# A two-layer decoder trunk on one core: products reordered around late inputs, rows of 1/rms made later, the convolution's diagonal blocks built on chip, eight small matmuls added

## The chip, the core and the metric

The kernel runs on one core of a Trainium2 chip. The metric is device time in microseconds (us) of one execution; lower is better. Engines are named as the profile names them: PE is TensorE's matmul, PEld its weight load, DVE is VectorE, ACT is ScalarE, POOL is GpSimd, SP is SyncE (here it only issues DMAs).

## What is computed

A sequence of 256 positions with 1024 channels passes through two layers, all in float32. Cut to its core:

```python
def half_step_swiglu(h, g, w_gate, w_up, w_down):
    hn = rms_norm(h, g)
    return h + 0.5 * ((silu(hn @ w_gate) * (hn @ w_up)) @ w_down)      # 1024 -> 2816 -> 1024

def conformer_conv_module(hn, w_pw1, b_pw1, conv_w, conv_b, ln_g, ln_b, w_pw2, b_pw2):
    a, gate = split(hn @ w_pw1 + b_pw1, 2)
    u = a * sigmoid(gate)
    u = causal_depthwise_conv(u, conv_w) + conv_b       # 31 taps, 1024 channels
    u = silu(layer_norm(u, ln_g, ln_b))
    return u @ w_pw2 + b_pw2

for layer in range(2):
    h = half_step_swiglu(h, ...)
    hn = rms_norm(h, mix_norm[layer])
    h = h + (hybrid_mixer(hn, ...) if layer == 0 else conformer_conv_module(hn, ...))
    h = half_step_swiglu(h, ...)
return rms_norm(h, final_norm)
```

`hybrid_mixer` is a sparse attention with an indexer beside a short gated convolution, behind one input projection and in front of one output projection.

## The kernel before

Everything is kept transposed: channels on the 128 partitions, the 256 positions along the free axis. A float32 product is made of three single-pass matmuls (`mm3`, lines 260 to 264): a number is split into a high part `hi` and a remainder `lo`, and `wh*ah + wh*al + wl*ah` are summed in PSUM. Each weight tile of 128x2048 is loaded by SP (line 77, buffer `raw`), its high part is made by ACT (line 111, `whi`) and its low part by DVE (line 122, `wlo`). The class `Stream` keeps the order of these tiles: `st.hi(n)` and `st.lo(n)` let ACT and DVE run n tiles ahead of PE, and a new load is issued when a `wlo` is done.

The order of work is written out by hand and is the program's order on each engine; each engine takes its queue strictly in order. A planner (`Side`) decides only between which products the small pieces of the attention and the convolution's taps are put, by costs that the code gives it (`did_pe`, `did_dve`).

Four feed-forward halves (`ffn`, numbered 0 to 3) carry most of the time; the hybrid mixer stands behind the first, the conformer behind the third. What the change touches:

- **1/rms.** The scale 1/rms of a normalisation is not applied to the input but to the products. `norm_cols` (lines 303 to 321) sums squares with small matmuls (line 313), DVE adds epsilon, POOL takes the power -0.5 (line 320, tile `rc`); `row_of` (lines 323 to 330) turns this column into a row with two matmuls (line 326) and ACT copies it to `rstd`. DVE multiplies the finished products by `rstd` when it takes them out of PSUM (lines 344, 351, 963, 968).
- **Start of ffn 1 to 3** (line 398): the products of the first two tiles run over inputs `xh[0..5]` first and over `xh[6..7]` afterwards, because the last pieces of x come late (ACT line 286, DVE line 287).
- **The conformer's convolution.** Channel tiles 0 and 1 are convolved by DVE: 30 taps each, one instruction a tap (line 930). Tiles 2 to 7 are convolved on PE (`conv_pe`, lines 882 to 891): 32 matmuls a tile in four column groups of 32, whose weights are diagonal 32x32 blocks (`W4`). The host packs these blocks and they are loaded by DMA, 512 KB a tile, three by SP ahead of the products and three by ACT between its other work (line 870). Their other operand `U4` is four shifted copies of the gated input u, written to DRAM by an ACT-issued DMA (line 877) and read back by four SP-issued DMAs (line 880) for each pair of tiles.
- **Behind it** comes the layer norm over 1024 channels: `shift_row` (line 907) makes a rough mean from two tiles on PE, DVE subtracts it (lines 901, 913), squares and sums are gathered on ACT, POOL and DVE (lines 916, 1021 to 1033), `cols` (line 921) sums them over channels on PE, and after the power on POOL (line 1053) two rows are made on PE (line 1058). Only then can the second pointwise product start (line 1074 on ACT makes its first input).

## Time and profile before

| | us |
|---|---|
| median of 3 runs | 957.34 |
| lowest and highest of the 3 | 947.97 and 966.21 |
| the profiled execution, its own time | 947.35 |
| its span in the trace | 945.6 |

The profile shows one execution, the 947.35 one. The page gives busy time and idle time of each engine; the list of waits says who waited for whom; the timeline gives start and duration of each instruction, with the idle time in front of it and what ended it in square brackets; the table of stretches gives busy time of each engine in a stretch, the number of instructions in it, and the clock that was granted to PE (1.00 is 2.4 GHz, 0.50 is 1.2 GHz).

### The profile page before, as it was taken

How to read it: one execution, taken by the hardware profiler on the slowest of the kernel's cores; microseconds unless marked ns; L12 is line 12 of the kernel's file. 1: busy time of each engine (PE TensorE's matmuls, PEld its weight loads, DVE VectorE, ACT ScalarE, POOL GpSimd, SP SyncE). 2: the span in 40 equal slices, each digit the busy share in tenths (PEclk: the TensorE clock that was granted, in tenths of full speed). 3: DMA queues.
4: the chain of work that ended last, by engine and by line, in shares of the span. 5: the costliest groups of instructions: out<-in, count | busy, mean ns of one | idle time of the engine just before them, and what ended most of it. 6: DMA issues, size and time to landing. Idle time of an engine off the chain costs nothing. (4 is left out here: it accounts for less than half of the span.)

```text
span 945.6 us, 18509 instructions
## 1 busy us (share of the span) xinstructions
PE 926.0 (98%) x8166; PEld 903.8 (96%) x8166; DVE 613.0 (65%) x684; ACT 445.6 (47%) x504; POOL 93.9 (10%) x77
## 2 busy tenths in 40 slices
PE   8999999999999999999999999999987999999997
PEld 8999999989989999999999999999964999999997
DVE  6776656669776766556666565665975776666542
ACT  7554434554664544344544443455441465444441
POOL 1000001233102000002310000023001020000011
PEclk9999999999999999999999999999998999999999
DMA  8565445672245555455755553568773265554641
GB/s 336 219 230 207 153 149 189 235 257 87 90 178 199 218 208 179 141 166 187 271 194 202 187 188 123 184 229 315 213 218 92 90 225 221 179 200 133 188 150 45
DMA packets 32961, 176.71 MB, mean 187 GB/s; under 512 B 3568, under 2 KB 7536, under 8 KB 18928
## 3 DMA queue, kind: packets, MB, share of 16 engines
q1 hardware_dynamic: 31056, 172.02, 52.2%
q10 hardware_dynamic: 1824, 3.50, 1.2%
q8 instruction: 64, 1.05, 0.4%
q14 instruction: 17, 0.14, 0.0%
HBM read 173.58 MB, written 1.93 MB: 186 GB/s over the span
## 5 line engine op out<-in xcount | busy, mean ns | idle before, releaser
L262 PE MATMUL acc<-xh,whi 128*128 128x256 f32 x1632 | 453.7, 278 | 1.5 <-ACT xh L286 1.5
L263 PE MATMUL acc<-xl,whi 128*128 128x256 f32 x1632 | 452.4, 277 | 1.0 <-DVE xl L287 0.7
L264 PE MATMUL acc<-xh,wlo 128*128 128x256 f32 x1632 | 452.0, 277 | 0.0
L122 DVE TENSOR_TENSOR wlo<-raw,whi 128x2048 fp32r<-128x2048 f32 (+2 forms) x175 | 364.7, 2098 | 11.4 <-ACT whi L111 11.3
L111 ACT ACTIVATE whi<-raw 128x2048 fp32r<-128x2048 f32 (+2 forms) x175 | 299.6, 1715 | 150.3 <-PE acc L263 95.5
L262 PEld LDWEIGHTS acc<-xh,whi 128*128 128x128 f32 x1632 | 307.5, 188 | 2.5 <-ACT xh L286 1.8
L263 PEld LDWEIGHTS acc<-xl,whi 128*128 128x128 f32 x1632 | 307.4, 188 | 1.8 <-DVE xl L287 1.8
L264 PEld LDWEIGHTS acc<-xh,wlo 128*128 128x128 f32 x1632 | 307.2, 188 | 0.0
L264 PE MATMUL acc<-hh,wlo 128*128 128x256 f32 x704 | 194.3, 276 | 0.0
L262 PE MATMUL acc<-hh,whi 128*128 128x256 f32 x704 | 194.3, 276 | 0.0
L263 PE MATMUL acc<-hl,whi 128*128 128x256 f32 x704 | 194.3, 276 | 0.0
L262 PEld LDWEIGHTS acc<-hh,whi 128*128 128x128 f32 x704 | 132.2, 188 | 0.0
L263 PEld LDWEIGHTS acc<-hl,whi 128*128 128x128 f32 x704 | 132.2, 188 | 0.0
L264 PEld LDWEIGHTS acc<-hh,wlo 128*128 128x128 f32 x704 | 132.2, 188 | 0.0
L345 ACT ACTIVATE gs<-gs 128x512 f32<-128x512 f32 x44 | 27.9, 634 | 142.4 <-DVE gs L344 142.4
L351 DVE TENSOR_TENSOR us<-acc,rstd 128x512 f32<-128x512 f32 x44 | 30.4, 690 | 93.5 <-PE acc L264 93.5
L300 POOL TENSOR_TENSOR sqsum<-sqsum,sq 128x256 f32<-128x256 f32 x35 | 54.5, 1558 | 144.4 <-ACT sq L292 143.9
L435 DVE SCALAR_TENSOR_TENSOR x<-acc,x 128x256 f32<-128x256 f32 x32 | 13.6, 425 | 80.3 <-PE acc L264 80.3
L286 ACT ACTIVATE xh<-x,par 128x256 fp32r<-128x256 f32 x48 | 23.8, 505 | 81.1 <-DVE x L435 63.0
L344 DVE TENSOR_TENSOR gs<-acc,rstd 128x512 f32<-128x512 f32 x44 | 30.4, 691 | 46.5 <-PE acc L264 40.4
L300 POOL TENSOR_TENSOR sqsum<-sq 128x256 f32<-128x256 f32 x6 | 5.2, 874 | 543.8 <-ACT sq L292 524.5
L287 DVE SCALAR_TENSOR_TENSOR xl<-x,par,xh 128x256 fp32r<-128x256 f32 x48 | 24.2, 512 | 18.7 <-ACT xh L286 18.7
(187 smaller groups left out, 668.3 us busy)
## 6 DMA issues: line engine op xcount, KB each, us to landing
raw<-in_wgu_dram SPq DMA_DIRECT2D x85, 1024.0 KB, 4.8
raw<-in_wdn_dram SPq DMA_DIRECT2D x64, 704.0 KB, 4.2
raw<-in_wp_dram SPq DMA_DIRECT2D x12, 1024.0 KB, 5.0
raw<-in_wcv_dram SPq DMA_DIRECT2D x6, 1024.0 KB, 4.8
raw<-in_wout_dram SPq DMA_DIRECT2D x4, 1024.0 KB, 4.8
u<-ud SPq DMA_DIRECT2D x12, 284.0 KB, 5.4
raw<-in_wgu_dram SPq DMA_DIRECT2D x4, 512.0 KB, 6.9
raw<-in_wzq_dram SPq DMA_DIRECT2D x2, 1024.0 KB, 5.0
```

Source lines behind the costliest of these rows:

```text
L111: self.nc.scalar.activation(hi[:, :n], self.raw[i][:, :n], AF.Copy)
L122: self.nc.vector.tensor_tensor(lo[:, :n], raw[:, :n], hi[:, :n].bitcast(FT), op=OP.subtract)
L262: nc.tensor.matmul(ps, wh, ah, start=start, stop=False, skip_group_check=skip)
L263: nc.tensor.matmul(ps, wh, al, start=False, stop=False, skip_group_check=skip)
L264: nc.tensor.matmul(ps, wl, ah, start=False, stop=stop, skip_group_check=skip)
L286: nc.scalar.activation(xh[:, d], x[:, d], AF.Copy, scale=g)
L287: nc.vector.scalar_tensor_tensor(xl[:, d], x[:, d], g, xh[:, d].bitcast(FT), op0=OP.mult, op1=OP.subtract)
L300: nc.gpsimd.tensor_tensor(total, parts[0], sq, op=OP.add)
L344: nc.vector.tensor_tensor(gs, two(G), bc2(rstd), op=OP.mult)
L345: nc.scalar.activation(gs, gs, AF.Silu)
L351: nc.vector.tensor_tensor(us, two(U), bc2(rstd), op=OP.mult)
L435: nc.vector.scalar_tensor_tensor(x[:, d], ps[:, :S], 0.5, x[:, d], op0=OP.mult, op1=OP.add)
```

## The change

Seven edits, in the order of the diff's core:

1. `settle`: eight matmuls of 32 columns of weights by 256 in the four column groups, their results unused, behind `row_of` of ffn 0; there `row_of` itself stands 24 matmuls later.
2. The start of ffn 1 to 3 runs over inputs 0 to 3, then 4 and 5, then 6 and 7.
3. `row_of` of the hybrid mixer stands behind the second half's products for both position blocks instead of between them; that of the conformer 12 matmuls later.
4. The diagonal blocks are built on chip from 256 more columns of the parameters: one multiplication of an identity pattern with the weights, both broadcast, 128x1024. Tiles 2, 3 and 4 are built by POOL behind `norm_cols`, tiles 5, 6 and 7 by DVE between the taps. The six loads of 512 KB are gone.
5. After the last pointwise product, `st.hi(3)` and `st.lo(1)` become `st.hi(2)`: the high part of one weight tile further ahead is made later.
6. The planner is told of the builds, and so puts other numbers of taps between the other instructions.
7. The sums for the layer norm: tile 6 is now added into the sums by DVE, and `cols` over the gathered sums stands behind the last convolution tile instead of in its middle.

```diff
+    def settle():
+        p = tp()
+        for _ in range(2):
+            for c in range(4):
+                nc.tensor.matmul(p[32 * c:32 * c + 32, :S], ones[:, :32], con[:, :S], start=True, stop=True,
+                                 tile_position=(0, 32 * c))
...
-                for k0, k1 in ((0, 6), (6, 8)):
+                for k0, k1 in ((0, 4), (4, 6), (6, 8)):
...
-                    if u == 1 and j == 0:
+                    if u == 1 and j == 0 and f:
                         rstd = row_of(rc)
                     run(0, 1, 0, 8, False)
+                    if u == 1 and j == 0 and not f:
+                        rstd = row_of(rc)
+                        settle()
...
-                    if h == 1 and b == 0:
+                    if h == 1 and b == 1:
                         rstd = row_of(rc)
...
+            def build_w4(ct, eng):
+                W4[ct] = cp.tile([128, 32, 32], FT, name="w4", bufs=3)
+                eng.tensor_tensor(W4[ct], m32[:, None, :].to_broadcast([128, 32, 32]),
+                                  par[:, P_W4 + 32 * ct:P_W4 + 32 * ct + 32][:, :, None].to_broadcast([128, 32, 32]),
+                                  op=OP.mult)
+                if eng is nc.vector:
+                    side.did_dve(1.2)
...
-                        if i == 0 and j == 1 and n == 7:
+                        if i == 0 and j == 1 and n == 11:
                             rstd = row_of(rc)
...
                         rc = norm_cols()
+                        for ct in (2, 3, 4):
+                            build_w4(ct, nc.gpsimd)
...
-                    st.hi()
-                    st.lo(1 if i == 3 else AHEAD)
+                    if (i, j) == (3, 1):
+                        st.hi(2)
+                    else:
+                        st.hi(3 if i == 3 else AHEAD)
+                        st.lo(1 if i == 3 else AHEAD)
...
-                load_w4(ct + 3)
+                build_w4(ct + 3, nc.vector)
...
-            nc.vector.tensor_tensor(sd[:, 0], sd[:, 0], sd[:, 1], op=OP.add)
+            nc.vector.tensor_tensor(sq, sq, q0, op=OP.add)
             conv_out(6, p6)
             last = pairs("sg")
             nc.scalar.activation(last[:, 0], v[:, 6], AF.Square)
-            nc.vector.tensor_tensor(sq, sq, q0, op=OP.add)
+            nc.vector.tensor_tensor(sd[:, 1], sd[:, 1], v[:, 6], op=OP.add)
+            nc.vector.tensor_tensor(sd[:, 0], sd[:, 0], sd[:, 1], op=OP.add)
+            nc.vector.tensor_tensor(sq[:, 1], sq[:, 1], last[:, 0], op=OP.add)
             nc.vector.tensor_tensor(sq[:, 0], sq[:, 0], sq[:, 1], op=OP.add)
             p, p2 = acc(), acc()
-
-            def early():
-                cols(p, sd[:, 0], True, False)
-                cols(p2, sq[:, 0], True, False)
-                cols(p, v[:, 6], False, False)
-                cols(p2, last[:, 0], False, False)
-
-            p7 = conv(7, early)
+            p7 = conv(7)
             conv_out(7, p7)
+            cols(p, sd[:, 0], True, False)
+            cols(p2, sq[:, 0], True, False)
```

PE's queue in ffn 0, where the row of 1/rms is made (`rc` is the column, `con` the constants), before:

```order
L263 MATMUL acc<-xl,whi 128x256
L264 MATMUL acc<-xh,wlo 128x256
L326 MATMUL tp<-con,rc 128x128 x2
L262 MATMUL acc<-xh,whi 128x256
L263 MATMUL acc<-xl,whi 128x256
L264 MATMUL acc<-xh,wlo 128x256
```

and with the change, 24 matmuls further on:

```order
L264 MATMUL acc<-xl,whi 128x256
L265 MATMUL acc<-xh,wlo 128x256
L327 MATMUL tp<-con,rc 128x128 x2
L338 MATMUL tp<-con,ones 32x256 x8
L263 MATMUL acc<-xh,whi 128x256
L264 MATMUL acc<-xl,whi 128x256
```

The row is followed by the eight matmuls of `settle`, then by the next products.

ACT's queue from the last write of u to DRAM on (`w` are the diagonal blocks, `v` the convolution's result), before:

```order
L877 DMA ud<-u 128x2x287
L111 ACTIVATE whi<-raw 128x2048
L985 ACT_TABLE_LOAD
L985 ACTIVATE dummy<-ones 128x1
L899 ACTIVATE v<-acc,par 128x256
L870 DMA w_7861<-in_w_dram 128x1024
L899 ACTIVATE v<-acc,par 128x256
L870 DMA w_7905<-in_w_dram 128x1024
L909 ACTIVATE shift<-tp 128x256
L870 DMA w_7958<-in_w_dram 128x1024
```

and with the change:

```order
L894 DMA ud<-u 128x2x287
L1003 ACT_TABLE_LOAD
L1003 ACTIVATE dummy<-ones 128x1
L914 ACTIVATE v<-acc,par 128x256 x2
L924 ACTIVATE shift<-tp 128x256
L931 ACTIVATE q<-v 128x512
```

The `whi` that stood in front of the two copies of the convolution's results is gone from here, and so are the three loads.

DVE's queue from the last gated input u on (`v<-u,par,v` are taps), before:

```order
L972 SCALAR_TENSOR_TENSOR u<-av,par,sg 128x256 x2
L930 SCALAR_TENSOR_TENSOR v<-u,par,v 128x256 x26
L901 SCALAR_TENSOR_TENSOR v<-acc,par,shift 128x256
L913 TENSOR_TENSOR v<-v,shift 128x512
L122 TENSOR_TENSOR wlo<-raw,whi 128x2048
L901 SCALAR_TENSOR_TENSOR v<-acc,par,shift 128x256
L930 SCALAR_TENSOR_TENSOR v<-u,par,v 128x256 x8
L913 TENSOR_TENSOR v<-v,shift 128x512
```

and with the change:

```order
L987 SCALAR_TENSOR_TENSOR u<-av,par,sg 128x256 x2
L945 SCALAR_TENSOR_TENSOR v<-u,par,v 128x256 x6
L884 TENSOR_TENSOR w_7868<-con,par 128x1024
L945 SCALAR_TENSOR_TENSOR v<-u,par,v 128x256 x6
L884 TENSOR_TENSOR w_7910<-con,par 128x1024
L945 SCALAR_TENSOR_TENSOR v<-u,par,v 128x256 x8
L916 SCALAR_TENSOR_TENSOR v<-acc,par,shift 128x256
L884 TENSOR_TENSOR w_7959<-con,par 128x1024
L928 TENSOR_TENSOR v<-v,shift 128x512
L123 TENSOR_TENSOR wlo<-raw,whi 128x2048
L916 SCALAR_TENSOR_TENSOR v<-acc,par,shift 128x256
L945 SCALAR_TENSOR_TENSOR v<-u,par,v 128x256 x14
```

The same 34 taps stand here, 20 instead of 26 in front of the first result that needs the shift, 14 instead of 8 behind it, and three builds among them.

## Rows read from the trace of the kernel before

**Rows 1.** The page: its first line, and PE's busy time.

```profile
span 945.6 us, 18509 instructions
...
PE 926.0 (98%) x8166; PEld 903.8 (96%) x8166; DVE 613.0 (65%) x684; ACT 445.6 (47%) x504; POOL 93.9 (10%) x77
```

**Rows 2.** A wait of PE: who waits for whom, us in total, times, longest.

```profile
PE tp L326 <- POOL rc L320: 1.0, 3, 0.6
```

**Rows 3.** Timeline of PE in the convolution: start, us, instruction, count, [idle before it].

```profile
705.45 1.13 PE L907 MATMUL tp<-v,ones 128*128 128x256 f32 x4 [2.44 <-ACT v L899]
706.51 3.66 PE L888 MATMUL acc<-u,w 128*32 128x256 f32 x64
716.01 8.15 PE L888 MATMUL acc<-u,w 128*32 128x256 f32 x96 [5.85 <-DVE v L930]
...
732.91 0.38 PE L262 MATMUL acc<-u,whi 128*128 128x256 f32 x1 [0.30 <-ACT u L1074]
```

**Rows 4.** Stretches of 1 us there; the third figure from the end is PE's clock.

```profile
715.00:716.00 1.00, 0.00 (x0) 0.02 (x1) 0.97 (x4) 0.00 (x0) 0.00 (x0) 0.50 0.91 352
...
721.00:722.00 1.00, 1.00 (x16) 0.56 (x12) 0.00 (x0) 0.00 (x0) 0.00 (x0) 0.67 0.00 0
```

**Rows 5.** Timeline of ACT in the convolution.

```profile
701.60 1.91 ACT L111 ACTIVATE whi<-raw 128x2048 fp32r<-128x2048 f32 x1 [10.10 <-DMA raw<-in_wgu_dram]
```

**Rows 6.** DMAs issued from 701 to 705 us, then from 689 to 693 us: KB, us to landing.

```profile
u<-ud SPq DMA_DIRECT2D x4, 284.0 KB, 9.2
...
u<-ud SPq DMA_DIRECT2D x4, 284.0 KB, 4.9
```

**Rows 7.** Timeline of DVE in the convolution.

```profile
692.54 0.69 DVE L968 TENSOR_TENSOR av<-acc,rstd 128x512 f32<-128x512 f32 x1 [3.17 <-PE acc L264]
...
694.14 10.38 DVE L930 SCALAR_TENSOR_TENSOR v<-u,par,v 128x256 f32<-128x256 f32 x26
707.03 0.48 DVE L901 SCALAR_TENSOR_TENSOR v<-acc,par,shift 128x256 f32<-128x256 f32 x1 [2.52 <-ACT shift L909]
...
708.03 2.29 DVE L122 TENSOR_TENSOR wlo<-raw,whi 128x2048 fp32r<-128x2048 f32 x1
...
710.64 5.26 DVE L930 SCALAR_TENSOR_TENSOR v<-u,par,v 128x256 f32<-128x256 f32 x8
...
727.97 0.48 DVE L901 SCALAR_TENSOR_TENSOR v<-acc,par,shift 128x256 f32<-128x256 f32 x1 [3.93 <-PE acc L888]
```

**Rows 8.** Timeline of POOL in the conformer.

```profile
653.65 2.71 POOL L320 TENSOR_TENSOR rc<-ms,halfm 128x2 f32<-128x2 f32 x1 [1.52 <-DVE ms L318]
710.87 1.37 POOL L1021 TENSOR_TENSOR sg<-v 128x512 f32<-128x512 f32 x1 [54.50 <-DVE v L901]
...
729.86 0.70 POOL L1053 TENSOR_TENSOR rs<-var,halfm 128x2 f32<-128x2 f32 x1 [16.22 <-DVE var L1051]
```

**Rows 9.** Stretches of products: us, then PE, PEld, DVE, ACT, POOL busy (count), clock.

```profile
477.00:480.80 3.80, 3.80 (x35) 3.80 (x34) 3.80 (x2) 3.21 (x2) 2.69 (x1) 1.00 0.18 28
482.00:652.00 170.00, 170.00 (x1502) 170.00 (x1501) 108.50 (x96) 79.62 (x77) 13.97 (x8) 1.00 0.56 196
734.00:757.00 23.00, 23.00 (x197) 23.00 (x197) 17.02 (x27) 11.15 (x24) 2.28 (x3) 1.00 0.27 95
780.00:920.00 140.00, 140.00 (x1238) 140.00 (x1237) 84.47 (x74) 63.57 (x60) 6.11 (x4) 1.00 0.53 181
```

**Rows 10.** Timeline of PE at the start of ffn 1.

```profile
286.40 0.38 PE L262 MATMUL acc<-xh,whi 128*128 128x256 f32 x1 [0.24 <-ACT xh L286]
286.92 0.38 PE L263 MATMUL acc<-xl,whi 128*128 128x256 f32 x1
...
287.87 0.39 PE L263 MATMUL acc<-xl,whi 128*128 128x256 f32 x1 [0.33 <-DVE xl L287]
```

**Rows 11.** Timeline of PE at the start of ffn 3.

```profile
757.74 0.28 PE L262 MATMUL acc<-xh,whi 128*128 128x256 f32 x1
758.17 0.38 PE L263 MATMUL acc<-xl,whi 128*128 128x256 f32 x1
```

More of the change, by code (lines that the diff above doesn't have):

```diff
@@ L48 @@
 P_W31 = 104
-P_HW = P_W31 + 8 * TAPS
+P_W4 = P_W31 + 8 * TAPS
+P_HW = P_W4 + 256
 NP = P_HW + 12
@@ L188, in trunk_kernel @@
 @with_exitstack
-def trunk_kernel(ctx: ExitStack, tc: tile.TileContext, xT, wfirst, wgu, wdn, wza, wzq, wcv, wout, wp1, w4, wp2,
+def trunk_kernel(ctx: ExitStack, tc: tile.TileContext, xT, wfirst, wgu, wdn, wza, wzq, wcv, wout, wp1, wp2,
                  params, consts, out):
@@ L865, in pcol @@
                 return par[:, o + i:o + i + 1]
-            def load_w4(ct):
-                t = cp.tile([128, 1024], FT, name="w4", bufs=3)
-                (nc.scalar if ct > 4 else nc.sync).dma_start(t, w4[ct - 2])
-                W4[ct] = t.rearrange("p (b c) -> p b c", b=32)
+            m32 = con[:, C_M32:C_M32 + 32]
+            def build_w4(ct, eng):
[5 more added lines that the diff above has]
+                    side.did_dve(1.2)
             def build_u4(i):
@@ L880, in build_u4, with conv_pe @@
                     nc.sync.dma_start(U4[i][32 * r:32 * r + 32], rows[:, :, r:r + LU])
-            def conv_pe(ct, between=None):
+            def conv_pe(ct):
                 ps = acc()
                 for q in range(8):
-                    if q == 4 and between:
-                        between()
                     for c in range(4):
@@ L933, in conformer @@
             rc = rstd = None
-            for ct in (2, 3, 4):
-                load_w4(ct)
             for i in range(4):
@@ L985, in conformer, with conv @@
             nc.scalar.activation(dummy, ones[:, :1], AF.Silu)
-            def conv(ct, between=None):
-                p = conv_pe(ct, between)
+            def conv(ct):
+                p = conv_pe(ct)
                 side.did_pe(3.5)
@@ L1005, in conformer @@
             conv_out(4, p)
-            load_w4(7)
+            build_w4(7, nc.vector)
             side.did_dve(0.4, True)
@@ L1011, in conformer @@
             n = st.nlo
-            st.hi(2)
             st.lo(2)
@@ L1234, in _pack @@
     w4[:TAPS] = cw
-    w4 = w4.reshape(8, 4, 8, 4, 32)[:, :, 2:].transpose(2, 1, 4, 3, 0)
-    blocks = np.zeros((6, 4, 32, 4, 8, 32), np.float32)
-    for c in range(32):
-        blocks[:, :, c, :, :, c] = w4[:, :, c]
-    blocks = blocks.reshape(6, 128, 1024)
+    w4 = w4.reshape(8, 4, 8, 4, 32)
+    par[:, P_W4:P_W4 + 256] = w4.transpose(1, 4, 2, 3, 0).reshape(128, 256)
     hw = a["hyb_conv_w"][0]
     par[:, P_HW:P_HW + 12] = hw.T.reshape(4, 128, 3).transpose(1, 0, 2).reshape(128, 12)
-    return dict(xT=xT, wfirst=wfirst, wgu=wgu, wdn=wdn, wza=wza, wzq=wzq, wcv=wcv, wout=wout, wp1=wp1, w4=blocks, wp2=wp2,
+    return dict(xT=xT, wfirst=wfirst, wgu=wgu, wdn=wdn, wza=wza, wzq=wzq, wcv=wcv, wout=wout, wp1=wp1, wp2=wp2,
                 params=par, consts=_constants())
```

## The prediction

> **What bounds the kernel.** I read the page first: PE is busy for 926.0 of 945.6 us [rows 1], so only three kinds of time can go: the 20 us in which PE idles, the stretches in which its clock is halved, and the pace at which it takes the products. The change removes almost no products, so I looked for these three one after the other.
>
> The list of PE's waits and its timeline put most of the idle time into the convolution of the conformer. PE waits 2.44 us before the shift row, then 5.85 us in front of the sixth convolution tile, and the second pointwise product starts at 732.91 [rows 3]. The table of 1 us stretches shows what the second wait costs on top: the granted clock is down to 0.50 (1.2 GHz) before PE is back, and is not full again until after 721 us [rows 4], so that 96 convolution matmul records take 8.15 us where 64 took 3.66 us before it, that is 5.5 us at the full clock [rows 3].
>
> Who is late? ACT's timeline: a `whi` stood 10.10 us in front of ACT's queue, waiting for a weight tile that is not needed before ffn 3 [rows 5]. Behind it are queued the table load, both copies of the convolution's results (for which the shift row waits) and the issue of two loads of diagonal blocks. PE's wait at 716.01 carries DVE's name, but that tile reads neither v nor any tap; it waits for the last copies `U4`. Issued at about 702 us together with the loads of blocks they took 9.2 us to land; the pair before took 4.9 us [rows 6].
>
> The third kind is seen in no list of waits. In long stretches of identical products the number of matmuls tells the pace. From 482 to 652 us there are 1502 in 170 us, less the two or three that overlap an edge: 113 ns each. From 780 to 920 us it is 113 ns again. But from 734 to 757 us it is 197 in 23 us, 118 ns, and from 477 to 480.8 us 117 ns, all at the full clock of 1.00 [rows 9]. So there are two paces, 4.3 ns apart, and the switch comes where the stream is broken: the short slow stretch lies between the sums of squares and the row of ffn 2, and the slow one after the convolution ends at a gap at 758.17 [rows 11]. In this execution all four feed-forward parts ran fast. A feed-forward part has 1584 product matmuls, 1464 of them behind its row, so a slow one costs 6.3 us. The three runs of before lie 18 us apart, which is about three such parts; the profiled one, 947.35 us, lies at their lower end, and 10 us under the median of 957.34.
>
> The Trainium skill (TensorE: Matmul & The Clock Gate, "Back-to-back issue gap") gives one gap for 256 columns at the full clock, N/2.4 + 2.5 = 109 ns, and no second pace. By that page the rival on paces below would not exist and the chance of my own case would rise; the trace disagrees, since 113 and 118 ns stand in it at the same clock.
>
> **The change, part by part,** against the profiled execution (span 945.6, time 947.35).
>
> *Convolution.* With the `whi` gone from ACT's queue, both copies run as soon as their tiles are done. Three tiles of 3.6 us [rows 3] from 692.4 end at 703.1, and the shift row starts there, 2.4 us sooner. Without 1.5 MB of blocks beside them, `U4` should take 4.9 instead of 9.2 us [rows 6], so the sixth tile starts by 711.7 and, two tiles of 3.6 us on, PE is done by 719.
>
> Then DVE is late next, and I follow its queue. It reaches the taps at 694.14 and takes 0.40 us each (10.38/26) [rows 7]. A build of 128x1024 is not in the trace; two SBUF operands of 128x2048 take 2.29 us [rows 7], half of the first is 1.15, and I take that. Twenty taps and two builds: 704.4. The shift row arrives 1.58 us after its start (705.45 to 707.03) [rows 3, 7]: 704.7. Take-out 0.4, third build 1.15, centring 0.6, `wlo` 2.2, take-out 0.4: 709.4. Fourteen taps are 5.6 us, but beside POOL's two adds eight taps took 5.26 instead of 3.2 us [rows 7], so 2.1 more: 717.1. Centring 0.6, two adds of 128x512 1.2, take-out 0.4, four adds of 128x256 at 0.4, and 0.3 for ACT's square in between: 721.2. There the last take-out starts, which started at 727.97 [rows 7]. From it to the first product it was 4.94 us [rows 3, 7], with the same small matmuls and the same power on POOL. So the product starts at about 726.1: **6.8 us sooner**.
>
> Two prices stand against it. PE now idles for 2 to 4 us before the sixth tile and again before the sums. Idle for 5.85 us cost it half its clock for 6.7 us, from 715.0 or before to 721.7 [rows 3, 4]; idle for 2.44 us did not. If it falls, up to 3.3 us of products are lost, otherwise nothing; I take the middle, **1.7 us**. POOL's three builds: 128x512 takes 1.37 us [rows 8], so 2.74 us each, 8.2 us from 656.4 on. DVE loses 2.1 us beside 2.8 us of POOL [rows 7, 8], so at most 6.1 us. DVE idles for 3.17 us before 692.54 [rows 7], which hides half; besides, the first builds fall on a time in which DVE waits for PE. Between 0 and 2.9 us remain; I take **0.9**.
>
> On this the Trainium skill (SBUF — State Buffer, "Who interferes with whom") says that a POOL instruction that reads SBUF and a DVE instruction with two SBUF inputs exclude each other for a whole instruction, whoever starts first. The trace agrees: the power of two columns takes 2.71 us while a `wlo` runs, and 0.70 us alone [rows 8]. By the page alone DVE could lose all 8.2 us, which would make the sum 2 us worse than my upper bound.
>
> The sums over tile 6 move from PE to DVE: two adds more, counted above. The `whi` taken out is made later, in the second pointwise product, in which ACT is busy for 11.15 of 23 us [rows 9]: nothing. If that cover were missing, ffn 3 would start 1.9 us later.
>
> *Starts of ffn 1 and 3.* Input 4 was needed after 12 matmuls (1.4 us) and is now needed after 48 (5.4 us). In ffn 1 five matmuls from 286.40 to 287.87 took 1.47 instead of 0.45 us, behind a wait of 0.24 [rows 10]: **1.3 us**. In ffn 3 the gap of 0.43 instead of 0.12 [rows 11]: **0.3 us**.
>
> *Rows later.* Three waits of PE for `rc`, **1.0 us** together [rows 2], go; POOL's 2.71 us for the power [rows 8] is what they waited for, and 12 to 24 further matmuls (1.4 to 2.7 us) cover it. DVE takes out the first products that much later; six PSUM buffers hold three tile pairs, 16 us, so PE does not wait. If it did, the cost would be the same 1.4 to 2.7 us.
>
> *settle.* Thirty-two such matmuls take 3.66 us [rows 3], eight take **0.9 us**, all on PE's path.
>
> Sum: 6.8 - 1.7 - 0.9 + 1.3 + 0.3 + 1.0 - 0.9 = 5.9 us, and 947.35 - 5.9 = **941.4 us**, provided that the four long parts keep the fast pace.
>
> **Rivals.**
>
> *One long part slow.* The gap at 758.17 that turned the last feed-forward part from slow to fast [rows 9, 11] is what the new order of products removes. If the products behind the convolution are slow again, the slow pace passes through the sums and the row (which switch twice) and stays: 1464 x 4.3 ns = 6.3 us, 947.7 us. The same if `settle` leaves ffn 0 slow. For it: 734 to 757 us was slow. Against it: the stage before it is timed anew.
>
> *From the hybrid mixer on.* With no waits left between the mixer and the conformer, ffn 1, ffn 2 and the first pointwise product share one pace: 3360 matmuls x 4.3 ns = 14.4 us, 955.8 us. For it: nothing is left that could switch back. Against it: the stretch before ffn 1 was fast in the profile.
>
> *All slow, the other side.* The waits that are removed also drew the pace afresh. Should every part get the slow one, from `settle` on, it is 6.3 + 14.4 + 6.3 = 27 us, 968.4 us: slower than the median of before by 1.2%. It decides at the first product behind `settle`, the mixer and the convolution.
>
> *The change doesn't do what it says:* `U4` lands as late as before, because the weight tile issued just ahead of it fills the DMA queues. Then PE is again the last in the convolution, the 6.8 us shrink to about 0.7, and it is 947.5 us.
>
> *Everything goes well:* the clock doesn't fall, POOL costs nothing, and the 200 products behind the convolution are fast (0.9 us): 937.9 us.
>
> **How the numbers follow.** Forecast 941.4 us: 0.34, own range 938.5 to 945. All well, 937.9: 0.18. One part slow, 947.7: 0.22. From the mixer on slow, 955.8: 0.13. Loads late, 947.5: 0.08. All slow, 968.4: 0.05. The range from 936 to 956 leaves out the last case, half of the one from the mixer on, and a little below. A measurement of this kernel can tell about 2% from no change, that is less than 938.2 or more than 976.5 us against 957.34. Most of "all well" and a small part of my own case lie below the first: faster 0.21. Only a still slower form of the last case lies above the second: 0.02. The rest, 0.77, is within 2%, although most of it lies below the median of before, because that median already holds slow parts.
>
> **What would show it.** In the profile of the changed kernel: no wait of ACT for a weight tile near 700 us; PE's shift row directly behind the third tile; the wait before the sixth tile under 4 us or gone; the last take-out near 721 us and the first product near 726 us; no gap in the first 84 matmuls of ffn 1 and 3; no wait for `rc` except in the conformer's norm; eight small matmuls near 27 us. The pace is read from counts: 113 ns in the four long parts makes my case; 118 ns in one names the rival. The prediction is wrong in its mechanism if the sixth tile still starts after 715 us, if DVE's builds or POOL's make PE wait for weights, or if the time goes down by more than 10 us against the profile.

## The result and the profile after

The changed kernel took 938.99 us (median of 6 executions, 937.72 to 954.27), the kernel before on the same chip 954.65 (6 executions, 947.97 to 966.21). The ratio of their times is 0.988, with a 95% interval from 0.984 to 0.993: about 1.2% shorter, and within the 2% that were called no change. (The ratio leaves disturbed executions out, the medians and the spans from lowest to highest do not.) The forecast was 941.4, in a range from 936 to 956.

The profiled execution took 938.84 us with a span of 937.0, against 947.35 and 945.6 before [rows 1]. That is 8.6 us of span. PE's idle time fell by 5.0 of them (from 19.6 to 14.6 us) and its busy time by 3.6; busy time includes matmuls that run at half the clock, as the 96 records in 8.15 us of before [rows 3].

The page of the changed kernel, its first line and PE's:

```profile
span 937.0 us, 18526 instructions
...
PE 922.4 (98%) x8174; PEld 903.4 (96%) x8174; DVE 618.4 (66%) x689; ACT 446.4 (48%) x504; POOL 97.5 (10%) x80
```

The list of PE's waits (us in total, times, longest us); the waits for `rc` of [rows 2] are not in it:

```profile
PE acc L936 <- DVE sg L1050: 3.3, 1, 3.3
PE acc L903 <- DMA u<-ud: 2.5, 1, 2.5
...
```

The timeline of PE in the convolution (start, us, instruction, count, idle before it and what ended it), which answers to [rows 3] (the profile has two records for each of these matmuls, so 64 for a tile of 32):

```profile
689.83 10.57 PE L903 MATMUL acc<-u,w 128*32 128x256 f32 x192
700.32 1.13 PE L922 MATMUL tp<-v,ones 128*128 128x256 f32 x4
701.38 3.66 PE L903 MATMUL acc<-u,w 128*32 128x256 f32 x64
707.51 7.11 PE L903 MATMUL acc<-u,w 128*32 128x256 f32 x128 [2.46 <-DMA u<-ud]
717.96 0.58 PE L936 MATMUL acc<-ones,sg 128*128 128x1 f32 x4 [3.33 <-DVE sg L1050]
...
725.35 0.78 PE L263 MATMUL acc<-u,whi 128*128 128x256 f32 x1
```

Three tiles run without a break, the shift row stands directly behind them, and the sixth tile waits 2.46 us where it waited 5.85. The last two tiles then run at full speed: 128 records in 7.11 us. A new wait of 3.33 us has come up in front of the sums, and DVE ends it. From the first tile to the first product it is 35.5 us (689.83 to 725.35), before it was 40.5 (692.43 to 732.91).

The four `u4` copies, issued now without blocks beside them, landed nearly as fast as the pair that was undisturbed before [rows 6] (issues from 699 to 709 us: KB, us to landing):

```profile
u<-ud SPq DMA_DIRECT2D x4, 284.0 KB, 5.1
```

DVE's timeline in the same place, against [rows 7]:

```profile
689.93 0.69 DVE L983 TENSOR_TENSOR av<-acc,rstd 128x512 f32<-128x512 f32 x1 [3.17 <-PE acc L265]
...
693.90 1.22 DVE L884 TENSOR_TENSOR w<-con,par 128x1024 f32<-128x1024 f32 x1
...
706.64 7.67 DVE L945 SCALAR_TENSOR_TENSOR v<-u,par,v 128x256 f32<-128x256 f32 x14
...
718.52 0.48 DVE L916 SCALAR_TENSOR_TENSOR v<-acc,par,shift 128x256 f32<-128x256 f32 x1
```

From `av` on DVE never idles until the last take-out: it is now what ends the stage. The take-out starts 28.7 us after the first tile, against 35.5 before.

The clock, in stretches of 1 us (the third figure from the end, as in [rows 4]):

```profile
719.00:720.00 1.00, 1.00 (x9) 1.00 (x10) 0.16 (x1) 0.42 (x1) 0.00 (x0) 0.85 0.00 0
720.00:721.00 1.00, 1.00 (x5) 1.00 (x6) 0.32 (x2) 0.00 (x0) 0.14 (x1) 0.50 0.06 16
...
726.00:727.00 1.00, 1.00 (x8) 1.00 (x8) 1.00 (x3) 0.97 (x3) 0.00 (x0) 0.74 0.00 0
```

It falls to 0.50 (1.2 GHz) among the small matmuls behind the 3.33 us wait, and in this execution not at the sixth tile. From the last take-out to the first product it is 6.83 us, and was 4.94 [rows 3, 7].

The long stretches of products, with the counts from which the pace follows, against [rows 9]:

```profile
28.00:190.00 162.00, 162.00 (x1432) 162.00 (x1431) 107.87 (x94) 78.34 (x73) 10.58 (x6) 1.00 0.57 197
299.00:473.00 174.00, 174.00 (x1538) 174.00 (x1537) 110.52 (x97) 80.78 (x77) 13.49 (x7) 1.00 0.58 204
480.00:650.00 170.00, 170.00 (x1502) 170.00 (x1501) 108.33 (x96) 80.00 (x76) 14.10 (x9) 1.00 0.56 195
763.00:928.00 165.00, 165.00 (x1458) 165.00 (x1457) 94.73 (x84) 71.01 (x70) 8.30 (x6) 1.00 0.48 167
...
270.00:293.00 23.00, 23.00 (x205) 23.00 (x204) 18.75 (x19) 17.13 (x24) 5.37 (x7) 1.00 0.47 172
727.00:757.00 30.00, 30.00 (x267) 30.00 (x266) 21.91 (x32) 19.07 (x31) 5.37 (x7) 1.00 0.30 106
```

All four long parts run at 113 ns (162 us for 1432 products less the two or three that overlap an edge, and so on). The fifth row holds the start of ffn 1 and the sixth that of ffn 3: 205 and 267 products at the same 113 ns, without a gap where [rows 10, 11] had one.

### The profile page after: what moved, and what is told of

Same layout as the page of the kernel before. It is cut to its first block, busy times and chain, and to the rows that moved or that the text cites. A ratio compares the mean times of both kernels' runs of the same rounds, so it can differ in the third digit from the quotient of the medians.

```text
span 937.0 us, 18526 instructions
## 1 busy us (share of the span) xinstructions
PE 922.4 (98%) x8174; PEld 903.4 (96%) x8174; DVE 618.4 (66%) x689; ACT 446.4 (48%) x504; POOL 97.5 (10%) x80
## 4 chain that ended last, share of the span: by engine, by line
PE 94%; DVE 2%; DMA 1%; issue 1%; ACT 0%; SPq 0%; POOLq 0%; POOL 0%; DVEq 0%; ACTq 0%
PE acc L263 29%; PE acc L264 29%; PE acc L265 29%; PE acc L903 1%; DMA raw<-in_wgu_dram 1%; DVE v L945 1%; PE acc L268 1%; PE acc L270 1%; PE acc L269 1%; DMA raw<-in_wfirst_dram 1%; PE acc L1076 0%; PE acc L662 0%; PE tp L314 0%; PE tp L691 0%; PE acc L707 0%
```

## The experiments

They ran in three sets, each on another chip, each beside the kernel before. That one's median was 944.58 us in the first set (11 executions from 943.16 to 959.16), 946.12 in the second (35, from 942.76 to 969.33) and 950.82 in the third (23, from 942.84 to 968.23). Two theories were to be told apart: the gain is that of the stages (convolution, starts, rows); or it is that of the pace, 113 or 118 ns a product, which each break of the stream may switch.

| kernel | set | median us | lowest to highest | ratio to before, 95% interval |
|---|---|---|---|---|
| a1_no_settle | 1 | 943.54 | 936.57 to 949.55 | 0.997 (0.993 to 1.002) |
| a2_settle_again | 1 | 945.83 | 939.71 to 948.51 | 1.000 (0.997 to 1.003) |
| a3_whi_back | 1 | 942.69 | 941.74 to 956.30 | 0.998 (0.995 to 1.002) |
| a4_blocks_by_dma | 1 | 942.21 | 936.91 to 947.89 | 0.997 (0.993 to 1.001) |
| a7_changed_again | 2 | 945.57 | 935.92 to 953.33 | 0.996 (0.993 to 1.000) |
| a5_warm | 2 | 944.16 | 935.61 to 952.25 | 0.994 (0.991 to 0.997) |
| a6_settle_ffn1 | 2 | 949.43 | 944.88 to 961.97 | 1.003 (1.000 to 1.007) |
| a8_input4_early | 2 | 947.59 | 939.39 to 954.47 | 0.997 (0.993 to 1.000) |
| a9_row0_back | 3 | 941.89 | 936.31 to 944.99 | 0.992 (0.988 to 0.995) |
| a10_taps_early | 3 | 936.28 | 935.53 to 943.59 | 0.990 (0.984 to 0.995) |
| a11_taps_row0 | 3 | 935.29 | 932.26 to 948.54 | 0.987 (0.981 to 0.992) |
| a12_conv_only | 3 | 953.55 | 940.38 to 971.00 | 1.001 (0.996 to 1.005) |

Every edit is against the changed kernel.

**The change once more (a7).** No edit.

> The changed kernel as it is, beside the kernel before on the same chip. If its gain is the three stages read from the profiles (start of the conformer 2.6, convolution 5.0, end 1.0 us), an execution with all long parts at 113 ns takes 937.5 to 939.5 us, and the kernel before, which took 944.58 us in the first set, is 5 to 9 us longer. The rival is that the 15.7 us between the first medians were the chip's: then the median here is no more than 3 us under that of before. In the trace: the conformer's first convolution matmul to its first pointwise product in 35.5 us within 1 us.

The median is 0.55 us under that of before, and by the ratio 0.4%: the rival's outcome. But the theory on the stages holds in the trace: 34.9 us from the first convolution matmul to the first product, and the shortest execution is 935.92 against 942.76. What takes the gain back stands in two rows of the profiled execution (943.92 us), the products ahead of the row of ffn 0 and those behind it:

```profile
21.00:25.00 4.00, 4.00 (x36) 4.00 (x36) 1.80 (x1) 1.92 (x1) 0.11 (x1) 1.00 0.59 209
28.00:196.00 168.00, 168.00 (x1429) 168.00 (x1428) 107.56 (x94) 77.80 (x73) 10.56 (x6) 1.00 0.54 191
```

1429 products in 168 us, less those at the edges, are 117.7 ns each, 4.4 more than in the trace above, and 1440 of them stand between the row and the end of ffn 0: 6.3 us. Without it this execution would be at 937.6. Ten of the twelve lie between 943.9 and 953.3 us. The kernel before lies within 4 us of its shortest in 19 of 35. So in the profiled execution the changed kernel paid most of its gain for a slow part; that the others did so too is suggested by their times and not shown, since only one of them was traced.

**The small matmuls behind the row of ffn 0 (a1, a2).** They go in the first, and come a second time, 48 products later, in the second.

```diff
                         rstd = row_of(rc)
-                        settle()
...
+                    if u == 1 and j == 1 and not f:
+                        settle()
                     st.pop()
```

> The changed kernel without the eight matmuls of settle; nothing else differs. Theory (each break of the product stream by small matmuls switches between the two paces): behind the row of ffn 0 the stream stays at 118 ns to its end, 1440 products x 4.4 ns = 6.3 us more, less 1.1 us of settle: about 944.2 against 939.0 us, and the count of matmuls from 30 to 190 us falls by 4%. Rival (the pace is drawn by chance at each break and settle is only work): 113 ns in some executions as before, and in those 937.9 us.

> The changed kernel with a second settle in ffn 0, 48 products behind the first. Theory (every break switches): the 48 products between run at 113 ns, all behind the second at 118 ns, 6.1 us more plus 1.1 us of work: about 946.2 against 939.0 us. Rival (settle puts the stream into the fast pace whatever it was before): 113 ns behind both, 940.1 us.

From a1, the products ahead of the row and behind it; from a2, those ahead of the row, between the two groups, and behind the second:

```profile
20.80:25.00 4.20, 4.20 (x39) 4.20 (x39) 2.26 (x1) 1.92 (x1) 0.56 (x1) 1.00 0.59 201
27.00:195.00 168.00, 168.00 (x1429) 168.00 (x1428) 108.66 (x95) 78.33 (x73) 10.57 (x6) 1.00 0.55 192
```

```profile
20.50:25.00 4.50, 4.50 (x42) 4.50 (x41) 2.29 (x1) 3.60 (x2) 0.62 (x1) 1.00 0.46 195
27.50:32.00 4.50, 4.50 (x42) 4.50 (x41) 4.40 (x4) 4.03 (x3) 0.00 (x0) 1.00 0.45 131
34.00:197.00 163.00, 163.00 (x1386) 163.00 (x1385) 101.50 (x90) 73.97 (x70) 10.56 (x6) 1.00 0.55 193
```

In the trace of a1, without the group, the row took the stream from 113 to 118 ns. In that of a2, with the group behind the row, it stayed at 113, and the second group alone took it to 118. So the group mostly undoes the switch of the row; it does not bring the fast pace. Over all fourteen traces, in ffn 0: the row alone switched in four of five (a1, a9, a11, a12; not in the trace of before, where PE waited 0.18 us for `rc` there), row and group together in one of nine. That one is the first trace of the changed kernel. Its products ahead of the row lie 118 ns apart (45 from the first to the last of these lines), and those behind the group 113:

```profile
20.62 0.28 PE L265 MATMUL acc<-xh,wlo 128*128 128x256 f32 x1
...
25.92 0.28 PE L265 MATMUL acc<-xh,wlo 128*128 128x256 f32 x1
```

What is left to chance is the pace behind the sums of squares of ffn 0: 113 in nine traces, 118 in five, the changed kernel's two among the five. These are single traces: two of the six executions of a1 (936.57 and 936.86 us) are 6 us shorter than its profiled one, as if ffn 0 had been fast in them. The group's own price is seen where the row starts: 1.54 us from there to the next product with it (26.03 to 27.57), 0.36 without (25.72 to 26.08): 1.2 us.

**The same group behind the row of ffn 1 (a6).**

```diff
                     if u == 1 and j == 0 and f:
                         rstd = row_of(rc)
+                        if f == 1:
+                            settle()
```

> Eight more small matmuls behind the row of ffn 1, as there are behind that of ffn 0. Theory: any group of small matmuls that breaks the stream of products may switch the pace between 113 and 118 ns, and nothing switches it back before the conformer's sums; behind the row and the group the products of ffn 1, ffn 2 and the first pointwise product, 3360, then run at the pace they did not have before, so 0.9 us for the group and 14.4 us for the pace where they ran fast: about 15 us more than the changed kernel in most executions. Rival: the small matmuls settle the pace at 113 ns, or have nothing to do with it; then it is 0.9 to 1.1 us more than the changed kernel and all stretches are at 113.

The long part of ffn 1 and then that of ffn 2:

```profile
301.00:482.00 181.00, 181.00 (x1540) 181.00 (x1539) 108.94 (x97) 80.11 (x76) 13.48 (x7) 1.00 0.54 191
487.00:657.00 170.00, 170.00 (x1502) 170.00 (x1501) 108.56 (x97) 79.16 (x76) 13.28 (x7) 1.00 0.56 197
```

The theory is right on the place and wrong on how far it reaches: 118 ns in ffn 1 (181 us, 1540), and 113 again behind the sums and row of ffn 2. So it costs 1.2 us for the group and 1548 x 4.4 ns = 6.8 us, 8.0 in all and not 15. The shortest execution is 9.0 us over that of the changed kernel in the same set. In all thirteen other traces this part ran at 113 ns.

**The old order at the starts of ffn 1 to 3 (a8).**

```diff
-                for k0, k1 in ((0, 4), (4, 6), (6, 8)):
+                for k0, k1 in ((0, 6), (6, 8)):
```

> The order of the first products of ffn 1 to 3 as it was before the change (inputs 1 to 6 of one output, then of the next); all else as changed. Theory by the stage: the waits at the starts of ffn 1 and ffn 3 are back, 1.3 and 0.3 us, so 1.6 us more than the changed kernel with the same paces. Rival: those gaps drew the pace afresh, and without them a slow pace passes through; then with them back the long parts of ffn 1 and ffn 3 differ in pace from the products ahead of them in some executions, and the time spreads by 6 to 14 us.

The products behind the convolution, those between the gap at the start of ffn 3 and the sums, and the long part of ffn 3:

```profile
728.00:750.00 22.00, 22.00 (x196) 22.00 (x195) 16.76 (x26) 12.57 (x23) 2.28 (x3) 1.00 0.26 96
752.60:759.60 7.00, 7.00 (x61) 7.00 (x61) 5.39 (x4) 6.33 (x6) 1.54 (x2) 1.00 0.27 70
...
766.00:936.00 170.00, 170.00 (x1446) 170.00 (x1444) 93.23 (x84) 70.64 (x69) 8.31 (x6) 1.00 0.46 158
```

The gap switches here: 113 ns ahead of it, 118 behind it and to the end (7.00 us for 61 products less two at the edges, and 170 for 1446). In the trace of before the same gap had turned 118 into 113 [rows 9, 11]. It does not always: in a12 a gap of the same kind, 0.43 us, left 118 at 118, and in the traces of before, a8 and a12 the gaps at the start of ffn 1 left 113 at 113. So taking the gap away removes one throw of the dice, in whichever direction. The medians of a8 and a7, 947.59 and 945.57, differ by 2.0 us, close to the 1.6 of the theory, but with twelve executions each and this spread that isn't shown by them.

**The weight tile back in ACT's queue (a3).**

```diff
-                    if (i, j) == (3, 1):
-                        st.hi(2)
-                    else:
-                        st.hi(3 if i == 3 else AHEAD)
-                        st.lo(1 if i == 3 else AHEAD)
+                    st.hi()
+                    st.lo(1 if i == 3 else AHEAD)
```

> The changed kernel with the old look-ahead behind the last pointwise product, so that the high part of the first tile of ffn 3 stands again in ACT's queue in front of the copies of the convolution's results; the blocks are still built on chip. Theory (that instruction and its tile's landing held the shift row): the copies start near 702 instead of 693.5 us, the shift row 3 us later, and all behind it: about 942 us. Rival (only the block loads cost, since without them the tile lands early): under 0.5 us, 939.0 to 939.5 us.

ACT's timeline, then PE's:

```profile
705.84 1.91 ACT L112 ACTIVATE whi<-raw 128x2048 fp32r<-128x2048 f32 x1 [10.32 <-DMA raw<-in_wgu_dram]
```

```profile
709.68 1.13 PE L922 MATMUL tp<-v,ones 128*128 128x256 f32 x4 [2.43 <-ACT v L914]
...
727.32 0.98 PE L936 MATMUL acc<-ones,sg 128*128 128x1 f32 x4 [6.01 <-DVE sg L1047]
```

The wait of ACT is back with its length (10.10 before [rows 5]), PE's wait for the shift row too (2.44 [rows 3]), and the stage takes 39.4 us, 3.8 more than after. In the medians of the set that doesn't show, since each mixes executions of both paces; it does in the shortest executions, 941.74 here against 936.57 and 936.91 in a1 and a4. The profiled execution is the longest, 956.30 us, because ffn 0, the products behind the convolution and ffn 3 are at 118 ns in it: 3180 products, 14.1 us. Without these it would be at 942.2, where four of the other five lie (941.74 to 942.86), so what the trace shows of the stage is not peculiar to it.

**The blocks loaded, as before (a4).**

```diff
+            for ct in (2, 3, 4):
+                load_w4(ct)
...
-                        for ct in (2, 3, 4):
-                            build_w4(ct, nc.gpsimd)
...
-                build_w4(ct + 3, nc.vector)
+                load_w4(ct + 3)
...
-            build_w4(7, nc.vector)
+            load_w4(7)
```

> The changed kernel with the diagonal blocks loaded by DMA as before, 6 x 512 KB, from the same places in the queues; the look-ahead stays the new one and DVE has no builds. Theory (the loads delay the shifted copies, but DVE ends the stage): the copies take about 9 us to land, the sixth tile starts 4 us later, DVE has 3.6 us less to do, and PE and DVE end the stage nearly together: 938.5 to 940 us. Rival (the loads were what cost): the sixth tile starts 7 us or more later and the last take-out with it, 942 us or more.

PE's timeline, and the last take-out in DVE's:

```profile
712.10 9.96 PE L898 MATMUL acc<-u,w 128*32 128x256 f32 x128 [6.92 <-DMA raw<-in_wgu_dram]
721.98 0.61 PE L931 MATMUL acc<-ones,sg 128*128 128x1 f32 x4
...
727.29 0.38 PE L263 MATMUL acc<-u,whi 128*128 128x256 f32 x1 [0.30 <-ACT u L1083]
```

```profile
722.12 0.48 DVE L911 SCALAR_TENSOR_TENSOR v<-acc,par,shift 128x256 f32<-128x256 f32 x1 [1.25 <-PE acc L898]
```

The sixth tile starts at 712.10, 4.6 us later than after, behind a wait of 6.92 us, and the copies took 7.1 us to land instead of 5.1. The last two tiles take 9.96 us instead of 7.11, more than half of that at a clock of 0.50, and the last take-out starts 32.2 us after the first tile, 3.5 later than after. But the stage grew by 1.8 us only (37.3). DVE, without its three builds, has been done when the tiles come, so no wait is left in front of the sums, and the small matmuls behind the take-out ran at the full clock: 5.17 us to the first product instead of 6.83. Either edit of the convolution gives a part of the 5.0 us; what ends the stage passes from the copies to DVE.

**Fillers to keep the clock (a5).** Five 128x256 matmuls in front of the sixth tile, seven behind the last.

```diff
+            idle = tp()
+            for _ in range(5):
+                nc.tensor.matmul(idle[:, :S], ones, con[:, :S], start=True, stop=True)
             p6 = conv(6)
...
+            idle = tp()
+            for _ in range(7):
+                nc.tensor.matmul(idle[:, :S], ones, con[:, :S], start=True, stop=True)
             cols(p, sd[:, 0], True, False)
```

> Five 128x256 fillers in front of convolution tile 6 and seven behind tile 7, into a PSUM tile that nothing reads. Theory: the fall of the clock to 0.50 behind the last convolution tiles comes from PE idling for 3.3 us in front of tile 6 and again in front of the sums, and costs the 1.9 us by which the last take-out to the first product grew (6.83 against 4.94 us). Then the clock stays above 0.90 through the small matmuls, and the kernel takes 1.5 to 2 us less than the changed one. Rival: the sums wait for DVE and POOL and not for PE's clock; then the stretch from the last take-out to the first product stays at 6.5 to 7 us, or the fillers themselves, at 0.45 us each, delay what they are to help, and the time is the same or up to 2 us longer.

```profile
726.00:727.00 1.00, 1.00 (x10) 1.00 (x10) 0.20 (x1) 0.42 (x1) 0.00 (x0) 1.00 0.07 16
727.00:728.00 1.00, 1.00 (x7) 1.00 (x7) 0.48 (x3) 0.00 (x0) 0.29 (x1) 0.64 0.00 0
728.00:729.00 1.00, 1.00 (x5) 0.91 (x4) 0.48 (x1) 0.00 (x0) 0.41 (x1) 0.50 0.00 0
```

PE now waits only 0.3 us in front of the sums, and the clock falls all the same, later: at about 727.3 us, after 2 us in which PE is counted as busy with matmuls of one column. The stage takes 35.5 us, as in the first profile of the changed kernel, and from the last take-out to the first product it is 6.06 us, not the 4.94 of before. The theory that the fall comes from PE's idle time in front of the sums does not stand.

**The row of ffn 0 back (a9), taps earlier (a10), both (a11).**

```diff
-                    if u == 1 and j == 0 and f:
+                    if u == 1 and j == 0:
                         rstd = row_of(rc)
                     run(0, 1, 0, 8, False)
-                    if u == 1 and j == 0 and not f:
-                        rstd = row_of(rc)
-                        settle()
...
-                                side.fill()
+                                side.fill(5 if (i, j, n) == (3, 1, 7) else 0)
```

> The row of ffn 0 where it was before the change (after the first 24 products behind the sums, with its wait for rc) and no small matmuls behind it; all else as changed. In the set before this one the kernel before was at its shortest times, 943 to 947 us, in two thirds of its executions, the changed kernel at its own, 936 to 939, only in two of twelve. Theory: the wait for rc in ffn 0 set the pace of the 1440 products behind it to 113 ns, and without it they keep the pace that the start of the kernel happened to draw; then this kernel takes 936 to 939 us in more than half of its executions, 6 us less in the median than the changed kernel. Rival: the pace of ffn 0 is drawn at the start whatever the row does; then the spread is that of the changed kernel, with medians within 2 us.

> The changed kernel, with six taps more on DVE in front of the last take-out of the first pointwise product, where DVE idles for 3.17 us, and six fewer before the sums. Theory: behind the sixth convolution tile DVE is what ends the stage; six of the fourteen taps that take 7.67 us there go, 2.4 to 3.3 us, so PE's wait in front of the sums falls from 3.3 to about 1 us, and the convolution, 34.9 to 35.5 us from its first matmul to the first pointwise product, takes 32 to 33 us. If PE's shorter idle also keeps its clock, up to 1.9 us more. Rival: the u4 copies end it; then the sums wait for PE's own tile 7, PE's wait at the sixth tile stays 2.5 to 2.8 us, and the gain is under 1 us.

> Both edits together: the row of ffn 0 where it was and no small matmuls behind it, and six taps earlier. If both theories hold, the shortest executions are at 933 to 936 us, more than half of all are there, and the kernel beats the changed one by 8 us in the median. If the pace of ffn 0 is drawn whatever the row does, the shortest are the same but the median is 2 to 4 us under the changed kernel's.

The theory of a9 fell. (The two thirds that it starts from are 19 of 35 in the list.) In its trace PE did not wait for `rc` in ffn 0 at all, and the row alone took 118 to 113 ns; in a11 and a12, with the same row, it took 113 to 118. Four of the twelve executions of a9 are under 938 us, not more than half.

The theory of a10 held. DVE's timeline and PE's:

```profile
685.31 4.05 DVE L945 SCALAR_TENSOR_TENSOR v<-u,par,v 128x256 f32<-128x256 f32 x10
690.14 0.69 DVE L983 TENSOR_TENSOR av<-acc,rstd 128x512 f32<-128x512 f32 x1 [0.79 <-PE acc L265]
...
707.08 5.30 DVE L945 SCALAR_TENSOR_TENSOR v<-u,par,v 128x256 f32<-128x256 f32 x8
```

```profile
707.68 7.11 PE L903 MATMUL acc<-u,w 128*32 128x256 f32 x128 [2.19 <-DVE v L945]
716.02 0.58 PE L936 MATMUL acc<-ones,sg 128*128 128x1 f32 x4 [1.23 <-DVE sg L1050]
...
723.95 0.50 PE L263 MATMUL acc<-u,whi 128*128 128x256 f32 x1
```

Six taps more fit into DVE's idle 3.17 us, eight instead of fourteen are left (5.30 instead of 7.67 us), and PE's wait in front of the sums shrinks from 3.33 to 1.23. The stage takes 33.9 us, 33.3 in a11, a little over the 32 to 33 expected. The clock still falls to 0.50 behind it, so the second part of the gain did not come. The medians, 936.28 and 935.29 us, are the lowest of all (of six and seven executions), and by the ratios they are 1.0 and 1.4% under the kernel before in the same set; the changed kernel didn't run in that set, so that they beat it is shown by the stage (33.9 and 33.3 against 34.9 and 35.5) and not by medians.

**The convolution alone (a12).** The rows and the starts of ffn 1 to 3 as before the change, no small matmuls.

```diff
-                for k0, k1 in ((0, 4), (4, 6), (6, 8)):
+                for k0, k1 in ((0, 6), (6, 8)):
...
-                    if u == 1 and j == 0 and f:
+                    if u == 1 and j == 0:
                         rstd = row_of(rc)
...
-                    if u == 1 and j == 0 and not f:
-                        rstd = row_of(rc)
-                        settle()
...
-                    if h == 1 and b == 1:
+                    if h == 1 and b == 0:
...
-                        if i == 0 and j == 1 and n == 11:
+                        if i == 0 and j == 1 and n == 7:
```

> Of the change only the convolution is left (blocks built on chip, whi and sums moved); the three rows, the first products of ffn 1 to 3 are where they were before, and there are no eight small matmuls. By the stages of the profiles the convolution is worth 5.0 to 5.6 us against the kernel before, where all long parts run at 113 ns, so the shortest executions are at 937 to 940 us where the kernel before has 943 to 946. Rival: the rows and starts carry more than I give them (2.6 us of start less 0.9 for the small matmuls); then the shortest are under 3 us below the kernel before.

Inconclusive. The shortest execution, 940.38 us, is 2.5 under the shortest of before in the set, which is the rival's figure, but only one of twelve is near it. In the profiled one (956.76 us) ffn 0 and ffn 3 are at 118 ns, and the stage takes 38.2 us, more than the 34.9 to 37.4 of the other traces with the same convolution. PE's timeline shows where it was lost, in front of the third tile:

```profile
705.93 3.66 PE L900 MATMUL acc<-u,w 128*32 128x256 f32 x64 [1.58 <-DMA u<-ud]
```

This tile waits for its copies of u, which were issued 0.7 us before the first tile (696.54 against 697.24), where in the first profile of the changed kernel they were issued 2.5 us before it; the write of u that they wait for took 8.3 us to land instead of 6.4. The shift row and DVE's take-outs are late by as much, the last one by 1.8 us, and from it to the first product it is 7.74 us instead of 6.83. So the length of the stage also depends on when these copies are issued.

## Why the prediction was right

The forecast was 5.9 us under the profiled execution of before; 8.5 us went (947.35 to 938.84). Its condition, all four long parts at the fast pace, was met in the profiled execution, and that was luck in part: ffn 0 came to 113 ns there by a switch that only one of nine traces with row and group shows.

- *The convolution.* The last take-out was to come 6.8 us sooner in the stage; it came 6.85 sooner (28.69 against 35.54 us from the first tile). The queue of DVE that was followed by hand gave each step within 0.2 us: builds of 1.22 us where 1.15 were taken, fourteen taps of 7.67 where 7.7 were. a3 and a4 show that both causes named were causes: `whi` in ACT's queue, and the blocks beside `u4`.
- *The price of the clock.* 1.7 us were taken as the middle between nothing and 3.3; the stretch from the last take-out to the first product grew by 1.9. In a4 it took 5.17 us at the full clock, so 1.7 of the 1.9 are the clock's. That a middle comes out so near is luck: in a7 the same stretch took 6.22 us. The place was only half right. In this execution PE kept its clock through the idle 2.46 us in front of the sixth tile and lost it among the small matmuls of the sums, and a5 shows it lost there with hardly any idle time before them. But in a8 and a9 it fell to 0.50 at the sixth tile too, behind waits of 2.33 and 2.51 us, so that such a wait can cost the clock; from a9, to be held against the 7.11 us above:

```profile
706.50 8.80 PE L900 MATMUL acc<-u,w 128*32 128x256 f32 x128 [2.51 <-DMA u<-ud]
```

- *POOL's builds.* 0.9 us were taken from the convolution, and there it was nothing: this term was mis-sized. The builds do hold up DVE where they run. POOL's timeline has them, and DVE's has a take-out beside them (two instructions, 2.38 us in place of 0.88 before):

```profile
654.12 5.67 POOL L884 TENSOR_TENSOR w<-con,par 128x1024 f32<-128x1024 f32 x3
```

```profile
658.09 2.38 DVE L987 SCALAR_TENSOR_TENSOR u<-av,par,sg 128x256 f32<-128x256 f32 x2
```

  But some 30 us later DVE idles for 3.17 us in front of `av` exactly as before, so the delay had been made up. Besides, a build took 1.9 us and not 2.74. The Trainium skill (SBUF — State Buffer, "Who interferes with whom") has a POOL instruction that reads SBUF and a DVE instruction with two SBUF inputs exclude each other; the 2.38 us agree with it, and the end of the convolution shows nothing of it.
- *What comes before the convolution.* 1.4 us (1.3 at ffn 1, 1.0 for the rows, less 0.9 for the group) were predicted; the convolution started 2.6 us sooner. The group cost more than taken, 1.2 us. What outweighs it lies between the sums of the mixer and those of ffn 1, which were 100.5 us apart and are 98.0: 2.5 us, the gap of ffn 1 and a wait for `rc` among them. How much of the rest is the pace of the mixer's short stretches was not told apart.
- *What comes behind it.* 0.3 us were predicted and 1.0 came, because the products behind the convolution ran at 113 and not at 118 ns: 0.9 us that stood only in the rival "everything goes well".
- *The rivals.* In this result they lost. But "one long part slow", put at 947.7 us, is near what most executions of a7 show on another chip: 943.9 to 946.4 us in seven of twelve, with ffn 0 as the part in the profiled one. Its mechanism at the other end is borne out as well: in the eleven traces without the gap at the start of ffn 3, the long part of ffn 3 has the pace of the products behind the convolution each time, 113 ns in eight and 118 in three (a3, a6, a11). From a6, these products and the long part:

```profile
737.00:768.00 31.00, 31.00 (x265) 31.00 (x265) 22.65 (x32) 19.41 (x31) 5.35 (x7) 1.00 0.30 105
774.00:944.00 170.00, 170.00 (x1445) 170.00 (x1445) 93.91 (x84) 70.69 (x69) 8.30 (x6) 1.00 0.47 161
```

  What draws the pace behind the convolution stays open. "From the hybrid mixer on" came in none of the fourteen traces: ffn 1 ran at 113 ns in every one but a6's, where a group had been added, and ffn 2 in all. The chance of 0.22 for the first was too small against 0.34 for the forecast, if another chip is to count as well.

The other 7 us between the medians of the first comparison (15.7 against 8.5 in the profiles) are not shown to be the change's: the profiled execution of before was already at the lower end of its own, and over 35 executions on another chip the medians lie 0.5 us apart.

## What to carry to other kernels

Follow the one queue that will end the stage next, instruction by instruction with the durations of its own rows; that gave 6.8 of 6.85 us here, and the next gain (a10) came from asking the same queue where it idles just before. Count products per stretch before giving a reason for a difference of a few us: here a pace that a handful of small matmuls switch was worth 6.3 us in one feed-forward part, where the profiles before and after differ by 8.5, and a single execution, or a median of six, can hide or feign it. A wait that is removed may also have been what drew that pace anew.

## What the runs showed that was not expected

- The pace of 256-column products at a granted clock of 1.00 has two values, 113.3 and 117.7 ns (162 us for 1432 and 168 us for 1429, less those at the edges), and holds over 1500 products and more. In ffn 0 the row, or the group of eight, switched it alone (four of five, and one of one); both together did in one of nine. In ffn 1 and ffn 2 the sums of squares and the row switched one after the other, 113 to 118 and back to 113, in every trace but a6's, which is why these parts came out fast. The Trainium skill (TensorE: Matmul & The Clock Gate, "Back-to-back issue gap") gives 109 ns for this width, by a formula that it calls that of an isolated matmul; it says that in a stream the weight loads set the spacing as well. Neither value here is 109 ns, and the prediction held that figure against the stream as if it were meant for one. What sets the pace inside the engine stays open.
- The clock fell to 0.50 while PE was counted as busy, among products of one column, after a wait of only 0.3 us (a5); in a4 it fell in the idle stretch of 6.92 us and the same sums then ran at 1.00.
- A build of 128x1024 from two broadcast operands took 1.22 us on DVE and 1.9 us (5.67/3) on POOL.
